# Joining the two runs of small matmuls of each head in a hybrid decoder step

## The chip, the cores and the metric

One core of one Trainium2 chip. The metric is the device time of one execution in microseconds (us), on the slowest core used, here the only one.

## The reference

One inference step of one decoder layer over 512 prompt tokens and 8 sample tokens (one new token for each of 8 sequences), model width 1024, all in float32. The layer has an HGRN2 branch (8 heads, keys and values of 128), an RG-LRU branch, a gated merge, and a feed-forward part of width 4096. What the change touches is HGRN2 alone:

```python
S_t = diag(f_t) S_{t-1} + k_t outer v_t,   o_t = S_t^T q_t          # per head, S is 128 x 128
# chunkwise, per chunk of the prompt:
A = einsum('bhtk,bhsk,bhtsk->bhts', qc, kc, decay)     # s <= t, decay = product of f between s and t
o = o_inter + einsum('bhts,bhsv->bhtv', A, vc)
```

For the prompt, the masked matrix A of each chunk of 128 tokens is wanted. For the 8 sample tokens, one step: the stored state is scaled by f, k outer v is added, and q is applied.

## The kernel before

Big products are float32 done as three rounded products (`products`, L112, instruction at L118): a weight tile of 128 columns is split by ScalarE (L84, the high part) and VectorE (L87, the low part), and one product of 128 output columns takes 48 matmuls of 260 columns into a PSUM tile of the pool pmm, of which there are two. Splits are made two weights ahead. `gemm` also emits the gates of RG-LRU that are pending (`blockdiag`, L779, which reads xcs, the split of xc, which the conv chain L793 to L797 makes), and whatever parts have been put off with `later(n, part)`: they are emitted after the n-th next product.

Heads come one after another, each with six big products: f, q, output gate and v of the head (`head`, L530), and two for RG-LRU. After the v product, `head_sample_v` (L557) transposes the sample part of v, stores it to DRAM (vd, L564) and loads it back broadcast over all partitions (vb, L566), both on the DMA queue of SyncE.

`head_prompt` (L586) builds A by levels. `level(b)` (L609) for b = 1, 2, 4 up to 64 makes from the level before it two rows of factors, q-like and k-like, multiplied by decay factors, by one VectorE multiply (L614) and one copy (L618; for b = 1 the copy is ScalarE's, L616). Levels 1 to 32 go to tiles named Y, of which RING = 4 are alive; level 64 overwrites X, the head's own q, k and q times f. Blocks of A with distance between b and 2b are products of a level's two rows. For small b they are 32 x 32 blocks on the diagonal, computed whole by `blocks` (L633) and selected by masks. `small` (L626) issues one such matmul of 32 output columns, with high priority (`SESSION`), ordered behind the one before it, so that the small ones of one run stand together on TensorE. A small matmul is two MATMUL entries in the trace.

There are two runs in each head:

- Run 1, 48 matmuls behind level 2: the diagonal and level 1 from X (L647, 64 columns each), and the blocks for 2 and 4. VectorE then multiplies by the diagonal's mask (L650) and selects levels 1, 2 and 4 (copy_predicated, L652) into a32.
- Levels 4 to 32 follow, then `head_sample` (L570): ScalarE scales the eight stored states (L573) and VectorE adds k outer v from vb (L574), in eight updates ordered behind level 32. Level 64 is ordered behind the last.
- Run 2, 56 matmuls, ordered behind level 64's copy (order alone): level 64's block from the level 32 tile (L665), the sample outputs from the states st (L669), the blocks for 8 and 16, and the block for 32 (L674). VectorE then selects levels 8 and 16 (L676), and ScalarE copies the other blocks into `at` (L678, L681) and the sample outputs out (L682).

The keys' transposes (L694) come three products later, the states' products (L704) and outputs (L717, L719) one product later each.

The order of each engine's instructions is fixed when the program is built: a planner takes estimated durations, and gives each engine the ready instruction of the highest priority next. An order dependency made with `behind` only fixes this order; data dependencies become semaphore waits on the chip. GpSimd's own DMA queue keeps its descriptors in a scratch area of each SBUF partition.

Of the kernel before, what the change touches and what calls it, by code (L numbers as in the profile page):

```python
# [6 lines left out]
F32 = mybir.dt.float32  # L7
# [4 lines left out]
OP = mybir.AluOpType  # L12
# [10 lines left out]
C = 128  # L23
NC = L // C
# [16 lines left out]
PAIR = "pair"  # L41
EARLY = 8
EARLY_PLACE = 4
RING = 4
FIRST = 3
BUFS = {"e": 6, "g": 6, "xb": 1, "xc": 2, "xcs": 2, "gate": 4, "ag": 2, "hs": 3, "y": 3, "ma": 8, "rs": 1, "sq": 1, "t": 6, "sqs": 2,
        "a": 16, "b": 16}
# [4 lines left out]
class Kernel:  # L52
# [533 lines left out]
    def head_prompt(self, h, f, X, q, v, og, st, vb, fkq):  # L586
        nc = self.nc
# [11 lines left out]
        a32 = self.hg.tile([128, NC, 32], F32, name="a32")  # L599
        at = self.at  # L600

        def view(t, first_q, first_k, step, n, b):

            return bass.AP(tensor=t.tensor, offset=t.offset + first_q,
                           ap=[t.ap[0], [T + first_k - first_q, 2], [step, n], [1, b]])

        levels, decay = [X], [f[:, :L], 0]

        def level(b):  # L609

            X, (tb, to), n = levels[-1], decay, L // (2 * b)
            Y = levels[0] if b == C // 2 else self.hg.tile([128, 2, T], F32, name="Y", bufs=RING)
            fac = bass.AP(tensor=tb.tensor, offset=tb.offset, ap=[tb.ap[0], [1, 2], [2, n], [0, b]])
            made = nc.vector.tensor_tensor(view(Y, b, 0, 2 * b, n, b), view(X, b, 0, 2 * b, n, b), fac, OP.mult)  # L614
            if b == 1:
                nc.scalar.copy(view(Y, 0, 1, 2, n, 1), view(X, 0, 1, 2, n, 1))  # L616
            else:
                made = nc.vector.tensor_copy(view(Y, 0, b, 2 * b, n, b), view(X, 0, b, 2 * b, n, b))  # L618
            t2 = tb.rearrange("p (n two) -> p n two", two=2)
            tn = T_[:, to:to + n]  # L620
            nc.vector.tensor_tensor(tn, t2[:, :, 0], t2[:, :, 1], OP.mult)
            levels.append(Y)
            decay[:] = tn, to + n
            return made

        def small(after, *args):  # L626
            with self.tc.high_priority(offset=SESSION):
                ins = nc.tensor.matmul(*args, start=True, stop=True)  # L628
            for x in after:
                self.behind(ins, x)  # L630
            after[:] = [ins]

        def blocks(after, p, c0, x):  # L633
            for c in range(NC):
                for j in range(4):
                    s = slice(c * C + 32 * j, c * C + 32 * j + 32)
                    small(after, p[32 * j:32 * j + 32, c0 + c * 32:c0 + c * 32 + 32], x[:, 1, s], x[:, 0, s])
            return p[:, c0:c0 + 128].rearrange("p (c t) -> p c t", c=NC)

        level(1)  # L640
        made = [level(2)]
        p = self.pps.tile([128, 512], F32, name="ps")
        for c in range(NC):
            for j in range(4):
                s = c * C + 32 * j
                o = p[32 * j:32 * j + 32, c * 64:c * 64 + 64].rearrange("p (x t) -> p x t", x=2)
                small(made, o, X[:, 1, s:s + 32], X[:, 0::2, s:s + 32])  # L647
        first = p[:, :256].rearrange("p (c x t) -> p c x t", c=NC, x=2)
        found = {1: first[:, :, 0], 2: blocks(made, p, 256, levels[1]), 4: blocks(made, p, 384, levels[2])}
        nc.vector.tensor_tensor(a32, first[:, :, 1], self.mdiag, OP.mult)  # L650
        for b in (1, 2, 4):
            nc.vector.copy_predicated(a32, self.masks[b], found[b])  # L652

        level(4)
        level(8)
        level(16)
        state = self.head_sample(h, st, vb, fkq, level(32))
        with self.urgent():
            made = [self.behind(level(64), state)]
        p = self.pps.tile([128, 512], F32, name="ps")  # L660
        p2 = self.ppt.tile([128, 512], F32, name="pt")
        for c in range(NC):
            for j in (0, 32):
                s = c * C
                small(made, p2[j:j + 32, c * 64:c * 64 + 64], levels[6][:, 1, s + j:s + j + 32],  # L665
                      levels[6][:, 0, s + 64:s + 128])
        for b in range(NB):
            j, c = 32 * (b % 4), 256 + 128 * (b // 4)
            small(made, p2[j:j + 32, c:c + 128], fkq[:, 2], st[:, b])  # L669
        found = {b: blocks(made, p, c0, levels[n]) for b, c0, n in ((8, 0, 3), (16, 128, 4))}  # L670
        for c in range(NC):
            for j in (0, 64):
                s = c * C + j
                small(made, p[j:j + 32, 256 + c * 32:288 + c * 32], levels[5][:, 1, s:s + 32], levels[5][:, 0, s + 32:s + 64])  # L674
        for b in (8, 16):
            nc.vector.copy_predicated(a32, self.masks[b], found[b])  # L676
        for j in (0, 64):
            nc.scalar.copy(at[j:j + 32, :, j + 32:j + 64], p[j:j + 32, 256:384].rearrange("p (c t) -> p c t", c=NC))  # L678
# [4 lines left out]
        X, tb = levels[-1], decay[0]  # L683
# [1010 lines left out]
def build(inputs):  # L1694
    import numpy as np
    import concourse.bacc as bacc

    nc = bacc.Bacc("TRN2", target_bir_lowering=False, num_devices=1)
    arrays, ins, outs = {}, {}, {}
    for name in _INS:  # L1700
        a = np.ascontiguousarray(inputs[name])
        arrays[f"in_{name}_dram"] = a
        ins[name] = nc.dram_tensor(f"in_{name}_dram", a.shape, mybir.dt.from_np(a.dtype), kind="ExternalInput").ap()
    for n, (name, shape) in enumerate(_OUTS):
        outs[name] = nc.dram_tensor(f"out_{n}_dram", shape, F32, kind="ExternalOutput").ap()
    with tile.TileContext(nc, schedule_with_timeline_sim=True) as tc, ExitStack() as ctx:
        Kernel(ctx, tc, ins, outs).run()
    return nc, arrays
# [8 lines left out]
```

## Time and profile before

| | |
|---|---|
| median of 3 runs | 1008.83 us (1008.13 to 1009.62) |
| the profiled execution, its own time | 1009.9 us |
| its span, first to last instruction | 1008.1 us |
| TensorE busy | 983.1 us, 98% |
| VectorE busy | 695.9 us, 69% |
| ScalarE busy | 515.6 us, 51% |
| small matmuls (L628) on the chain that ended last | 1% on ps tiles, 1% on pt tiles |

In the profile PE is TensorE's matmul, PEld its weight load, DVE VectorE, ACT ScalarE, POOL GpSimd, SP SyncE. A q behind an engine's name means its sequencer or its DMA issue. A row of the timeline gives start, length, engine, line, operation, output and inputs, shape and count, and in brackets the idle time of the engine before it with what ended it. Matmuls are pipelined, so the lengths of neighbours overlap, and starts tell more than lengths.

### The profile page before, as it was taken

The page shows a single profiled execution, that of the slowest core. Times are in us where ns is not written, and L with a number is a line of the kernel's source. Part 1 is how long each engine was busy: PE and PEld are TensorE (multiplying, and loading weights), DVE is VectorE, ACT ScalarE, POOL GpSimd, SP SyncE. Part 2 cuts the span into 40 slices and gives each one's busy share as a digit, 9 for nine tenths or more (in the row PEclk, how much of TensorE's full clock was granted, in tenths as well). Part 3 has the DMA queues.
Part 4 walks back from the last instruction along what each step waited for, and adds up shares of the span by engine and source line. Part 5 has one row for each costly group of instructions (what it writes and reads, how often), then busy time and mean ns, then how long its engine had stood idle before and what let it go on. Part 6 is the DMA issues. An engine that isn't in the chain of part 4 may idle for free.

```text
span 1008.1 us, 23268 instructions
## 1 busy us (share of the span) xinstructions
PE 983.1 (98%) x9585; PEld 956.5 (95%) x9585; DVE 695.9 (69%) x1548; ACT 515.6 (51%) x986; POOL 112.6 (11%) x194
## 2 busy tenths in 40 slices
PE   5999999999999999999999999999999999999996
PEld 3799999999999999999998999999999999999996
DVE  6768888698878868463233338667767776777686
ACT  5444764574565456351122224466555645656664
POOL 3000000000000000120000000022321331232151
PEclk9899999999999999999999999999999999999998
DMA  9794444354444434586666756322762483274242
GB/s 301 214 259 135 121 129 149 94 147 131 113 126 122 119 94 131 186 267 210 190 189 195 241 165 181 99 85 53 155 170 64 98 197 104 54 170 93 63 85 85
DMA packets 212572, 145.78 MB, mean 145 GB/s; under 512 B 6262, under 2 KB 196878, under 8 KB 212458
## 3 DMA queue, kind: packets, MB, share of 16 engines
q1 hardware_dynamic: 202562, 132.37, 44.5%
q0 software_dynamic: 9904, 11.92, 6.3%
q8 instruction: 75, 1.23, 0.5%
q14 instruction: 31, 0.25, 0.1%
HBM read 123.61 MB, written 13.39 MB: 136 GB/s over the span
## 4 chain that ended last, share of the span: by engine, by line
PE 90%; DVE 3%; DMA 3%; SPq 2%; ACT 1%; issue 1%; DVEq 0%; ACTq 0%
PE mm L118 65%; PE ps L1151 8%; PE pt L1151 4%; PE ps L382 2%; PE pb L1151 2%; PE pb L779 1%; PE ps L628 1%; DMA wm<-in_w_mod_dram 1%; PE pt L704 1%; DMA xT_d<-ma 1%; SPq L75 1%; PE pt L717 1%; DMA wst<-in_w_in_dram 1%; DMA vb<-vd 1%; PE pt L628 1%
## 5 line engine op out<-in xcount | busy, mean ns | idle before, releaser
L118 PE MATMUL mm<-h,whi 128*128 128x260 f32 (+1 forms) x3072 | 508.3, 285 | 1.9 <-ACT X L157 1.2
L118 PEld LDWEIGHTS mm<-h,whi 128*128 128x128 f32 x3072 | 426.2, 189 | 6.7 <-ACT whi L84 1.7
L118 PE MATMUL mm<-h,wlo 128*128 128x260 f32 (+1 forms) x1536 | 314.6, 284 | 0.0
L84 ACT CAST whi<-wst 128x1024 fp32r<-128x1024 f32 x166 | 173.6, 1048 | 208.1 <-PE mm L118 171.2
L87 DVE TENSOR_TENSOR wlo<-wst,whi 128x1024 fp32r<-128x1024 f32 x166 | 202.6, 1221 | 90.4 <-ACT whi L84 89.3
L118 PEld LDWEIGHTS mm<-h,wlo 128*128 128x128 f32 x1536 | 239.8, 189 | 0.1
L118 PE MATMUL mm<-a,whi 128*128 128x260 f32 x512 | 82.8, 283 | 0.0
L118 PEld LDWEIGHTS mm<-a,whi 128*128 128x128 f32 x512 | 70.3, 188 | 0.9 <-issue 0.8
L118 PE MATMUL mm<-a,wlo 128*128 128x260 f32 x256 | 51.7, 284 | 0.0
L1247 DVE TENSOR_TENSOR f<-f 128x260 f32<-128x260 f32 x64 | 27.3, 427 | 28.9 <-ACT f L1242 28.2
L880 POOL DMA_DIRECT2D t<-oaT_d x8 | 4.3, 551 | 375.8 <-PE mm L118 368.8
L1239 POOL TENSOR_TENSOR ft<-ft,fsh 128x8 f32<-128x8 f32 x28 | 18.5, 660 | 215.5 <-DVE ft L1233 215.5
L1236 ACT ACTIVATE ft<-ft,fsh 128x512 f32<-128x512 f32 (+2 forms) x36 | 24.0, 676 | 35.9 <-DVE ft L1233 35.9
L118 PE MATMUL mm<-b,whi 128*128 128x260 f32 x256 | 41.6, 284 | 0.0
L118 PEld LDWEIGHTS mm<-a,wlo 128*128 128x128 f32 x256 | 39.4, 188 | 0.0
L118 PEld LDWEIGHTS mm<-b,whi 128*128 128x128 f32 x256 | 35.0, 188 | 2.5 <-issue 2.5
L614 DVE TENSOR_TENSOR Y<-Y,tb 128x512 f32<-128x512 f32 x40 | 27.5, 688 | 11.0 <-ACT Y L616 5.5
L896 DVE TENSOR_TENSOR t<-mm,t 128x520 f32<-128x520 f32 x8 | 5.6, 700 | 37.0 <-PE mm L118 37.0
L1284 POOL DMA_DIRECT2D ma<-snap x28 | 26.5, 948 | 40.1 <-issue 22.3
L1263 POOL DMA_DIRECT2D ma<-snap x28 | 26.6, 950 | 38.6 <-DMA ma<-snap 22.8
L1242 ACT ACTIVATE f<-ft 128x520 f32<-128x520 f32 (+1 forms) x36 | 20.8, 587 | 15.0 <-POOL ft L1240 13.0
L573 ACT ACTIVATE st<-st,fkq 128x128 f32<-128x128 f32 x64 | 19.6, 389 | 13.9 <-DVE fkq L553 12.8
(477 smaller groups left out, 1824.0 us busy)
## 6 DMA issues: line engine op xcount, KB each, us to landing
wst<-in_w_in_dram SPq DMA_DIRECT2D x64, 512.0 KB
wm<-in_w_mod_dram SPq DMA_DIRECT2D x8, 2048.0 KB
wst<-in_w_ff_dram SPq DMA_DIRECT2D x64, 256.0 KB
wst<-in_w_ff_dram SPq DMA_DIRECT2D x32, 512.0 KB
wm<-in_w_mod_dram SPq DMA_DIRECT2D x8, 1024.0 KB
st<-in_state_hgrn_dram SPq DMA_DIRECT2D x8, 512.0 KB
vb<-vd SPq DMA_DIRECT2D x8, 512.0 KB
out_dram<-st SPq DMA_DIRECT2D x8, 512.0 KB
```

The lines of the kernel that those rows point to most:

```text
L84: ins = self.nc.scalar.copy(hi, st)
L87: ins = self.nc.vector.tensor_tensor(lo, st, hi.bitcast(F32), OP.subtract)
L118: self.last_product = self.nc.tensor.matmul(ps[:, s, :c.stop - c.start], x, y[:, c], start=first and n == 0, stop=last and n == 2)
L382: ins = nc.tensor.matmul(ps[r:r + 32, j * n:j * n + n], self.cT[:, k, :], w[:, k, :], start=k < 4, stop=k >= KO - 4)
L614: made = nc.vector.tensor_tensor(view(Y, b, 0, 2 * b, n, b), view(X, b, 0, 2 * b, n, b), fac, OP.mult)
L628: ins = nc.tensor.matmul(*args, start=True, stop=True)
L1151: ins = self.nc.tensor.matmul(ps, x[:, w], y[:, f], start=j in (1, 7, 2) and k == 0 and n == 0, stop=k == 3 and n == 2, skip_group_check=True)
L1236: nc.scalar.activation(t[:, :p], t[:, :p], AF.Relu, bias=sh[:, 0:1])
L1242: nc.scalar.activation(f, self.two(self.ft)[:, a:a + n], AF.Square)
L1247: self.nc.vector.tensor_tensor(f[:, n], f[:, a], f[:, b], op)
L1263: nc.gpsimd.dma_start(x[1][:, b], v[:, :n], accum_op=OP.add)
L1284: nc.gpsimd.dma_start(x[t][:, a], s[p], accum_op=OP.add)
```

## The change

Run 1's matmuls move behind the state update and become one run with run 2's: first level 64's block, then the sample outputs, then the diagonal and level 1, the blocks for 2, 4, 8 and 16, and the block for 32. The run is ordered behind the last state update only, no longer behind level 64; level 64 is emitted behind the run (it overwrites X, which the run reads). The multiply by the diagonal's mask and all five selections come behind it. So six level tiles must be alive at once: RING goes from 4 to 6, and the scratch area of GpSimd's DMA queue is set to 8192 bytes a partition to make room.

```diff
-RING = 4
+RING = 6
+SCRATCH = 8192
...
-        level(1)
-        made = [level(2)]
-        p = self.pps.tile([128, 512], F32, name="ps")
-        for c in range(NC):
-            for j in range(4):
-                s = c * C + 32 * j
-                o = p[32 * j:32 * j + 32, c * 64:c * 64 + 64].rearrange("p (x t) -> p x t", x=2)
-                small(made, o, X[:, 1, s:s + 32], X[:, 0::2, s:s + 32])
-        first = p[:, :256].rearrange("p (c x t) -> p c x t", c=NC, x=2)
-        found = {1: first[:, :, 0], 2: blocks(made, p, 256, levels[1]), 4: blocks(made, p, 384, levels[2])}
-        nc.vector.tensor_tensor(a32, first[:, :, 1], self.mdiag, OP.mult)
-        for b in (1, 2, 4):
-            nc.vector.copy_predicated(a32, self.masks[b], found[b])
-
-        level(4)
-        level(8)
-        level(16)
+        for b in (1, 2, 4, 8, 16):
+            level(b)
         state = self.head_sample(h, st, vb, fkq, level(32))
-        with self.urgent():
-            made = [self.behind(level(64), state)]
-        p = self.pps.tile([128, 512], F32, name="ps")
+        made = [state]
         p2 = self.ppt.tile([128, 512], F32, name="pt")
...
-        found = {b: blocks(made, p, c0, levels[n]) for b, c0, n in ((8, 0, 3), (16, 128, 4))}
+        p = self.pps.tile([128, 512], F32, name="ps")
+        for c in range(NC):
+            for j in range(4):
+                s = c * C + 32 * j
+                o = p[32 * j:32 * j + 32, c * 64:c * 64 + 64].rearrange("p (x t) -> p x t", x=2)
+                small(made, o, X[:, 1, s:s + 32], X[:, 0::2, s:s + 32])
+        first = p[:, :256].rearrange("p (c x t) -> p c x t", c=NC, x=2)
+        found = {1: first[:, :, 0], 2: blocks(made, p, 256, levels[1]), 4: blocks(made, p, 384, levels[2])}
+        p = self.pps.tile([128, 512], F32, name="ps")
+        found |= {b: blocks(made, p, c0, levels[n]) for b, c0, n in ((8, 0, 3), (16, 128, 4))}
...
-        for b in (8, 16):
+        with self.urgent():
+            self.behind(level(64), state)
+        nc.vector.tensor_tensor(a32, first[:, :, 1], self.mdiag, OP.mult)
+        for b in (1, 2, 4, 8, 16):
             nc.vector.copy_predicated(a32, self.masks[b], found[b])
...
-    nc = bacc.Bacc("TRN2", target_bir_lowering=False, num_devices=1)
+    nc = bacc.Bacc("TRN2", target_bir_lowering=False, num_devices=1, dynamic_dma_scratch_size=SCRATCH)
```

## The prediction

> **What bounds the kernel now.** I read the page first (share of each engine, the chain that ended last), then busy time by stretch, then the waits of TensorE, and then the timeline around the two runs of small matmuls.
>
> ```profile
> PE 983.1 (98%) x9585; PEld 956.5 (95%) x9585; DVE 695.9 (69%) x1548; ACT 515.6 (51%) x986; POOL 112.6 (11%) x194
> ```
> ```profile
> PE 90%; DVE 3%; DMA 3%; SPq 2%; ACT 1%; issue 1%; DVEq 0%; ACTq 0%
> ```
>
> TensorE is the bound: 98% of the span, 90% of the chain. The stage of the change is the eight heads, from about 43 to 400 us. Columns below: stretch, length, then each engine's busy time.
>
> ```profile
> 66.00:86.00 20.00, 19.22 (x341) 18.60 (x339) 13.62 (x37) 6.42 (x12) 0.00 (x0) 1.00 0.62 173
> 86.00:110.00 24.00, 24.00 (x202) 24.00 (x203) 21.52 (x61) 15.02 (x39) 0.00 (x0) 1.00 0.36 101
> ...
> 130.00:400.00 270.00, 269.63 (x3338) 267.08 (x3338) 221.10 (x593) 155.25 (x332) 0.00 (x0) 1.00 0.42 122
> ```
>
> From 86 us on TensorE has no gap worth the name (269.63 of 270), so a microsecond taken off it there is a microsecond of the result, and so is one in which it waits. The one gap between 66 and 86 us (0.78) is this wait, whose matmul starts at 85.90:
>
> ```profile
> 85.90 0.39 PE L779 MATMUL pb<-xcs,bdhlru_wa 128*128 128x260 f32 x1 [0.78 <-ACT xcs L183]
> ```
>
> VectorE is at 82% in 130 to 400 us (221.10 of 270): busy, not the bound.
>
> **The change, part by part. The edges of a run.** Head 0's two runs on TensorE (start, length, line, count; one small matmul is two entries):
>
> ```profile
> 68.93 0.52 PE L118 MATMUL mm<-h,whi 128*128 128x260 f32 x3
> 69.38 0.65 PE L628 MATMUL ps<-X 128*32 128x64 f32 x32
> 69.85 0.74 PE L628 MATMUL ps<-Y 128*32 128x32 f32 x64
> 70.53 0.39 PE L118 MATMUL mm<-h,whi 128*128 128x260 f32 x1
> 70.75 0.40 PE L118 MATMUL mm<-h,wlo 128*128 128x260 f32 x2
> ...
> 80.11 0.28 PE L118 MATMUL mm<-h,wlo 128*128 128x260 f32 x1
> 80.31 0.58 PE L628 MATMUL pt<-Y 128*32 128x64 f32 x14
> ...
> 80.79 0.61 PE L628 MATMUL pt<-st,fkq 128*32 128x128 f32 x14
> 81.15 1.16 PE L628 MATMUL ps<-Y 128*32 128x32 f32 x80
> 82.24 0.39 PE L118 MATMUL mm<-h,wlo 128*128 128x260 f32 x1
> 82.46 0.64 PE L118 MATMUL mm<-h,whi 128*128 128x260 f32 x4
> ```
>
> In the big products one matmul follows another every 0.12 us (202 in 24.00 us from 86 to 110 us). Three of these at 68.93 put the last at 69.17, and the run starts 0.21 later. Within it the small ones start every 0.011 us (96 from 69.38 to 70.39, the last being 0.20 long). From the last small one to the next big one passes 0.14, and from that to the one after it 0.22 (70.53 to 70.75). The edges so take 0.21 + 0.14 + 0.22 = 0.57 us. Without the run two ordinary steps of 0.12 and, in the joined run, one small step of 0.01 stand there: 0.25. Run 2's edges are alike (0.20, 0.13, 0.22). **Joining saves 0.32 us a head, 2.5 us over eight.** The 104 small matmuls themselves stay as they are, in another order. I see no reason for another price: from both sides 0.25 to 0.40 a head (2.0 to 3.2).
>
> **Where the joined run lands.** Today run 2 is ordered behind level 64's copy; the new one only behind the last state update, and it takes the first run's work with it. So the state update now decides when 104 matmuls go, and TensorE stops there if the state is late. VectorE in head 0:
>
> ```profile
> 66.77 0.28 DVE L562 COPY vs<-ps 8x128 f32<-8x128 f32 x1 [2.22 <-PE ps L560]
> ```
> ```profile
> 74.37 0.42 DVE L618 COPY Y<-Y 128x512 f32<-128x512 f32 x1
> 77.32 0.62 DVE L574 SCALAR_TENSOR_TENSOR st<-vb,fkq,st 128x128 f32<-128x128 f32 x2 [2.53 <-DMA vb<-vd]
> 77.85 0.30 DVE L652 COPY_PREDICATED a<-mask,ps 128x128 f32<-128x128 uint8 x1
> 78.05 1.66 DVE L574 SCALAR_TENSOR_TENSOR st<-vb,fkq,st 128x128 f32<-128x128 f32 x6
> ```
> ```profile
> 82.77 0.41 DVE L618 COPY X<-Y 128x512 f32<-128x512 f32 x1
> ```
>
> The order was planned with vb there when level 32 was done (74.79, end of the first L618 row); on the chip it came 2.53 us later, and all VectorE work behind it slid. Run 2, planned behind level 64's copy, started at 80.31, while that copy ended at 83.18; less the 2.53 it would have ended at 80.65. So plan and chip agree within 0.34 us but for that DMA. Today it costs no wait at run 2, because the run does not really need the copy, and its place was late enough for the state (79.71).
>
> In the joined kernel the state can be planned sooner: level 16 no longer waits for run 1 to free its buffer (six buffers), the mask selections are gone from between the updates, so vb alone sets it. Planned end of the state: vb at 74.8 or before, plus eight updates. They take 2.2 us here (77.32 to 79.71 less a 0.2 mask selection), so 77.0 or before. On the chip vb stays at 77.3 (its issue, below, hangs on weight loads and not on the run), so the state ends at 79.5. The last small matmul that reads it stands 0.8 us into the run (80.31 to 81.15), so the stall is 79.5 - (77.0 + 0.8) = 1.7 us at least. At most: vb planned as soon as the later heads have it, which is 6.8 us after the issue of vd:
>
> ```profile
> 67.08 0.29 SPq L564 DMA_DIRECT2D vd<-vs  x1
> 71.28 0.53 SPq L566 DMA_DIRECT2D vb<-vd  x1
> ```
> ```profile
> 112.41 0.33 SPq L564 DMA_DIRECT2D vd<-vs  x1
> 114.80 0.34 SPq L566 DMA_DIRECT2D vb<-vd  x1
> ```
> ```profile
> 119.21 0.61 DVE L574 SCALAR_TENSOR_TENSOR st<-vb,fkq,st 128x128 f32<-128x128 f32 x2
> ```
>
> 67.08 + 6.8 = 73.9, so 0.9 sooner, and up to 0.9 more if the plan is more hopeful than any head: a stall of 3.5. From the other side, nothing if other VectorE work is put ahead of the updates. I take 2.3, near the end that rows give. Of it 0.8 comes back: the matmul at 85.90 today waits 0.78 for the slid chain, and a TensorE 2.3 us later no longer does. **Head 0 pays 2.3 - 0.8 = 1.5 us.**
>
> **Heads 1 to 7.** In head 1 vb landed by 119.21, at most 6.8 us after vd was issued, against 10.2 in head 0 (later issue, slower transfer) and against the at most 7.7 that the plan trusted there. VectorE waited for vb once only (row below). So I take nothing here. From the other side: if the plan trusts vb as much too early as in head 0, each pays 2.5 - 0.8 = 1.7 us, 12 us in all.
>
> ```profile
> DVE st L574 <- DMA vb<-vd: 2.5, 1, 2.5
> ```
> ```profile
> DVE Y L614 <- PE ps L628: 5.5, 6, 1.5
> ```
>
> **The rest, beside TensorE.** The last row is the wait of level 16 for run 1; it goes. In its place level 64, which overwrites X, waits for the joined run's 32 entries that read X: they end some 1.3 us into the run (0.84 for the first two groups, 0.47 for these), so about 1.3 us a head instead of 0.9. Behind it on VectorE stand weight splits and the conv chain; the splits run two weights ahead (two big products, 11.6 us), so nothing. K, level 64's product, is transposed not before the third big product after the head's last; today its copy ends at 83.18, 2.9 us after run 2 begins, and only the last head waits for it:
>
> ```profile
> PE pt L694 <- DVE X L618: 0.4, 1, 0.4
> ```
>
> The new copy comes some 3 us after the start of an earlier run (an estimate: 1.3, then a multiply and a copy), so nothing, or that 0.4 again. The mask selections (five of 0.30, and one multiply) move behind the run; their reader, the output product, stands five big products behind the head. ScalarE's copy of p behind them waits today already; its cover is the second accumulator, one big product of 48 matmuls, 5.8 us. The two ps banks are held together; their next user is the next head. The smaller DMA scratch touches GpSimd's queue only: it is idle in this stage, and in the feed-forward part TensorE does not wait for it, so nothing.
>
> **Sum.** -2.5 + 1.5 = -1.0 us. Against the profiled execution's 1009.9 (span 1008.1) that is 1008.9; that execution is 1.1 above the median 1008.83, so I predict 1007.8. 0.2% (2 us) is about what this measurement tells from no change.
>
> **Rivals.** *Full gain:* the update is planned late enough, because VectorE is at 82% and its other work goes first; head 0 does not wait and the 0.8 at 85.90 partly goes: -2.5 to -3.2, 1006.0. For it: in head 0 today's state ends 0.6 us before run 2 (79.71, 80.31) in spite of its late vb. Against it: the high priority with which these matmuls are placed.
>
> *Slower, the state is late in the later heads:* place, the first matmul on st; price 1.7 us each as above; it decides from 0.15 us a head to undo the forecast, from 0.45 to make the kernel slower by 2 us; 1010.9 to 1020. For it: freed of the buffer wait, every head's update now hangs on vb alone, as head 0's does today. Against: vb is quicker there than in head 0 by 3.4 us.
>
> *Slower, the clock.* TensorE's granted clock fell after its pause at the start (the column behind the brackets):
>
> ```profile
> 20.00:24.00 4.00, 1.42 (x28) 0.59 (x20) 4.00 (x9) 2.96 (x6) 0.00 (x0) 1.00 1.14 321
> 24.00:28.00 4.00, 1.97 (x13) 1.20 (x17) 4.00 (x12) 1.10 (x2) 0.00 (x0) 0.62 1.09 349
> 28.00:31.00 3.00, 3.00 (x29) 1.41 (x22) 2.68 (x9) 1.83 (x4) 0.00 (x0) 0.50 1.09 348
> 31.00:35.00 4.00, 4.00 (x36) 3.78 (x40) 2.01 (x10) 1.59 (x4) 0.00 (x0) 0.90 1.09 347
> ```
>
> Some 4.6 us idle in eight (2.58 and 2.03) were followed, and overlapped, by half clock for 3.0 + 3.0 + 0.8 = 6.8 us, 3.4 us of work lost. If head 0's stall comes near 3.5 and sets that off: -2.5 + 3.5 - 0.8 + 3.4 = +3.6, 1012.4. The Trainium skill ("TensorE: Matmul & The Clock Gate", Part 1: The HAM clock gate) has the rate halved after one idle window of about 3.4 us; by that rule my 2.3 us sets off nothing and only the longest stall would. The trace agrees in kind, with its idle time broken up.
>
> *No gain at the edges:* the joined run is broken up by big matmuls while single updates are awaited; each break costs the 0.32 again: 1008.8 or a little over. Today's run 2 is whole in spite of the same eight updates.
>
> **How the numbers follow.** Forecast (head 0 takes back over half; edges broken up in part belongs here): 0.43, 1006.8 to 1009.5. Full gain: 0.32, 1005.6 to 1006.8. Late states: 0.17. Clock: 0.08. So faster 0.32, same 0.43, slower 0.25. Range 1005.6 to 1012.4: it leaves out the greater part of the late states and little else. The forecast's own range is 1006.8 to 1009.5.
>
> **What would show it.** One run of 208 entries a head instead of 96 and 112; TensorE's busy time less by some 2.5 us; a new TensorE wait at a matmul on st in head 0 of 1.7 to 3.5 us, with an idle VectorE ahead of it waiting for vb; none at 85.90. VectorE's wait for run 1 gone, one at level 64 instead. It is wrong if waits on st show up in several heads, or none in head 0, or if the edges of the joined run cost more than 0.57.

## The result and the profile after

| | before | changed |
|---|---|---|
| median | 1008.83 us (1008.13 to 1009.62) | 1025.74 us (1023.47 to 1029.83) |
| span of the profiled execution | 1008.1 us | 1025.9 us |

The changed kernel is slower: the ratio is 1.0171 (95% interval 1.0156 to 1.0186), 17 us. The forecast was 1007.8 with a range to 1012.4. It was wrong, and by a mechanism that none of its rivals named.

The page of the changed kernel: busy time, TensorE's granted clock in 40 slices, and the queue that brings instructions (packets, MB, share).

```profile
PE 986.0 (96%) x9585; PEld 959.2 (94%) x9585; DVE 694.0 (68%) x1548; ACT 515.6 (50%) x986; POOL 112.0 (11%) x194
PEclk9999999999899998999999999999999999999998
q8 instruction: 75, 1.23, 0.5%
```

TensorE executes the same number of instructions as before and is busy about as long (983.1 before), so the 17.8 us of span are time in which it stood still or ran on a lower clock. The stage says where. Columns as in the prediction:

```profile
66.00:86.00 20.00, 17.75 (x316) 16.31 (x314) 14.10 (x37) 6.27 (x11) 0.00 (x0) 1.00 0.68 185
...
130.00:400.00 270.00, 262.00 (x3286) 259.71 (x3289) 211.93 (x577) 150.61 (x323) 0.00 (x0) 0.99 0.42 121
```

From 130 to 400 us TensorE had 0.4 us idle before and has 8.0 now. Its waits (what was waited for, total, times, longest):

```profile
PE ps L629 <- issue: 10.2, 4, 4.2
...
PE pt L690 <- DVE tb L622: 1.3, 2, 1.0
PE pt L629 <- issue: 1.3, 1, 1.3
...
PE pb L775 <- ACT xcs L184: 1.0, 1, 1.0
```

The first row is new and the largest part of the matter. L629 is the small matmul, and "issue" says that TensorE waited for nothing that the profile shows: no semaphore, no operand. The four places on the timeline, in heads 2, 3, 4 and 7, with the rows ahead of two of them:

```profile
171.38 0.93 PE L629 MATMUL ps<-Y 128*32 128x32 f32 x76
173.06 0.88 PE L629 MATMUL ps<-Y 128*32 128x32 f32 x66 [0.75 <-issue]
...
224.99 0.57 PE L629 MATMUL ps<-Y 128*32 128x32 f32 x30 [1.27 <-issue]
...
260.18 1.49 PE L629 MATMUL ps<-Y 128*32 128x32 f32 x135
265.62 0.42 PE L629 MATMUL ps<-Y 128*32 128x32 f32 x7 [3.95 <-issue]
...
406.26 0.42 PE L629 MATMUL ps<-Y 128*32 128x32 f32 x6 [4.23 <-issue]
```

Each lies in the middle of matmuls on tiles of the same names; by the run's order in the program the matmul just before the stop was reading the same level (the blocks for 8, 16, 32 and 32). In head 4 only 7 of the run's 208 MATMUL rows are left when it comes. Heads 1, 5 and 6 run through without a stop. The two long stops are followed by a lower clock (the column behind the brackets; each row begins where a stop ends):

```profile
265.60:272.50 6.90, 6.88 (x40) 6.82 (x40) 1.48 (x6) 1.26 (x4) 0.00 (x0) 0.57 0.02 4
...
406.20:413.10 6.90, 6.84 (x42) 6.78 (x43) 2.70 (x7) 2.53 (x5) 0.00 (x0) 0.62 0.12 42
```

That costs 6.9 x 0.43 + 6.9 x 0.38 = 5.6 us of work. The account: stops 10.2, clock 5.6, the late state in head 0 1.3 + 1.3 (below), the waits at L690 0.9 more than at the same transposes before (1.3, 0.4), less the 2.5 forecast for the edges: +16.8 of the 17.8. The rest was not followed up.

**Two theories.** Instructions reach TensorE by the queue q8: 75 packets of 1.23 MB in all, so 16.4 KB each. TensorE's 9585 + 9585 entries in 75 packets are 256 to a block, 64 bytes each. A small matmul in float32 is two matmul and two weight-load entries: a run of 104 is 416 entries of this stream (entries count both from here on). The big products use 2 x 202 entries in 24 us (17 per us, a block in 15 us), a run that is not stopped 416 in 2.85 us (146 per us).

- *F (feeding):* the run outpaces the blocks. Counted in the trace's records (with TensorE's 82 semaphore and drain instructions), all four stops fall at the same place modulo 256, at 192 to within one entry. Each ends 1.3 to 1.5 us after a block of q8 has landed, by the queue's packet times: in head 2 the block landed 0.5 us before the stop began, in head 3 as it began; in head 4 it starts 1.4 us into the stop, at 263.02, lands at 264.14, and TensorE resumes at 265.62; in head 7 the three times are 403.73, 404.79 and 406.26. A run of 192 or 224, as before, never used up what had landed. By the counts, with k blocks landed, TensorE gets to entry 256k + 448 and no further, so whether a run of 416 passes depends on where in a block it starts: it should pass from about 185 to 255 and from 0 to 32 (modulo 256), and stop elsewhere unless the block comes early.
- *S (the run itself):* the joined run, its six level tensors or an operand or transfer in just these heads stops TensorE; the number of entries and their place in the blocks do not matter.

The Trainium skill ("Runtime: NRT & Kernel Launch", Instruction fetch mechanics) describes refills in blocks of 16 KiB, 256 instructions, and the trace agrees (16.4 KB, 256). It also holds that fetching is hidden because dispatch is slower than the refill; at some 150 entries per us the trace disagrees, by 10.2 us.

### The profile page after: what moved, and what is told of

Same layout as the page of the kernel before. It is cut to its first block, busy times and chain, and to the rows that moved or that the text cites. A ratio compares the mean times of both kernels' runs of the same rounds, so it can differ in the third digit from the quotient of the medians.

```text
span 1025.9 us, 23249 instructions
## 1 busy us (share of the span) xinstructions
PE 986.0 (96%) x9585; PEld 959.2 (94%) x9585; DVE 694.0 (68%) x1548; ACT 515.6 (50%) x986; POOL 112.0 (11%) x194
## 3 DMA queue, kind: packets, MB, share of 16 engines
q8 instruction: 75, 1.23, 0.5%
## 4 chain that ended last, share of the span: by engine, by line
PE 85%; DVE 5%; DMA 4%; SPq 3%; issue 2%; ACT 0%; DVEq 0%; ACTq 0%
PE mm L119 62%; PE ps L1147 8%; PE pt L1147 4%; PE pb L1147 2%; PE ps L383 2%; SPq L372 2%; DMA wm<-in_w_mod_dram 1%; DMA vb<-vd 1%; PE pb L775 1%; PE ps L629 1%; DVE wlo L88 1%; SPq L76 1%; PE pt L713 1%; PE pt L700 1%; DMA xT_d<-ma 1%
## 5 line engine op out<-in xcount | busy, mean ns | idle before, releaser
L158 ACT ACTIVATE gate<-pb,pa 128x260 f32<-128x260 f32 x32 | 15.3, 477 | 25.9 <-PE pb L775 25.7
```

## The experiments

Each is compared with runs of the kernel before on the same chip (medians 1009.3, 1010.0 and 1009.4 us in the three groups).

### A shorter joined run

The changed kernel without the blocks for 2 and 4, so 288 entries in a run; their part of A is left out.

```diff
-        found = {1: first[:, :, 0], 2: blocks(made, p, 256, levels[1]), 4: blocks(made, p, 384, levels[2])}
+        found = {1: first[:, :, 0]}
...
-        for b in (1, 2, 4, 8, 16):
+        for b in (1, 8, 16):
             nc.vector.copy_predicated(a32, self.masks[b], found[b])
```

> The joined run without the blocks for 2 and 4 (that part of A is left out): 72 matmuls a head, 288 entries of TensorE's stream instead of 416. Theory F (instruction blocks): TensorE's instructions come in 16 KB blocks of 256 entries on DMA queue q8, and in the changed kernel it stopped each time 64 entries short of a block's end, when the next block was late; a run of 288 is hardly longer than the 284 to 404 that it did without a stop. So the four waits inside the run (10.2 us) and the two stretches at half clock behind the long ones (6.8 us) go, and the work left out is 8 x 64 x 0.011 = 5.6: 1025.7 - 22.6 = 1003 us, between 1001.5 and 1006. Theory S (the run waits for data: a level's tile, a PSUM bank, the late states): the blocks for 8, 16 and 32, in which it stopped, are all still there with what they read, so the waits stay and only the work goes: 1020 us.

Measured: 1008.28 us (1007.27 to 1010.27), ratio 0.9989 (0.9979 to 0.9999). The four stops are gone; of what is left of TensorE's waits at the heads' work in this kernel, the two longest and one inside a run:

```profile
PE pt L629 <- issue: 1.5, 1, 1.5
PE pb L775 <- ACT xcs L184: 1.5, 1, 1.5
...
PE ps L629 <- issue: 0.5, 1, 0.5
```
```profile
342.00:349.00 7.00, 5.54 (x31) 5.34 (x32) 6.40 (x20) 2.35 (x6) 0.00 (x0) 0.76 0.28 77
```

The first is head 0's late state (on pt, at the state's products). The last is a short stop inside a run, in head 7, again at 192 modulo 256: the run starts at 173, and by F's count 275 of its 288 entries were at hand until the block that landed at 389.73. S fails: the blocks for 8, 16 and 32, where the stops were, are all there, and so are the six tensors. F is right on the four stops and some 5 us too low on the total, outside its range (to 1006). Part of that is in these rows: TensorE now waits 1.5 us for ScalarE's xcs in head 6, and behind that wait the clock fell (7.0 x 0.24 = 1.7 us).

### A longer second run in the kernel before

The two runs and the four level tensors of before, and 48 repeated matmuls at the end of run 2, into columns that nothing reads; run 2 so has 416 entries.

```diff
             for j in (0, 64):
                 s = c * C + j
                 small(made, p[j:j + 32, 256 + c * 32:288 + c * 32], levels[5][:, 1, s:s + 32], levels[5][:, 0, s + 32:s + 64])
+        for _ in range(3):
+            blocks(made, p, 384, levels[4])
```

> The kernel before with its two runs, and behind run 2 of each head 48 repeated matmuls (the blocks for 16, three times, to spare columns of PSUM), so that run 2 has 416 entries of the stream, as the joined run has; no order around it is changed. Work added: 8 x 96 x 0.011 = 8.4 us. Theory F: run 2 now starts, counted modulo 256 in TensorE's stream, at 236, 61, 8, 71, 20, 83, 32, 91 for heads 0 to 7; a run of 416 that starts between about 33 and 185 must stop for a block. So heads 1, 3, 5 and 7 stop at 192 (modulo 256), 1.5 to 4 us each, heads 0, 2, 4 do not, head 6 is on the edge; with one to four stretches at half clock (3.4 each): 1017 + 6 to 16 + 0 to 14, 1023 to 1040, most likely 1030. Theory S: these matmuls read tiles that are done and wait for nothing: 1017.2 us, no wait inside the runs.

Measured: 1039.19 us (1036.96 to 1042.27), ratio 1.0300 (1.0279 to 1.0320). The instruction queue, the waits put down to issue, and the stops of this kernel:

```profile
q8 instruction: 81, 1.33, 0.5%
```
```profile
PE ps L628 <- issue: 10.0, 4, 3.1
...
PE mm L118 <- issue: 3.0, 2, 2.0
PE pb L781 <- issue: 2.0, 1, 2.0
```
```profile
138.37 0.44 PE L628 MATMUL ps<-Y 128*32 128x32 f32 x14 [2.28 <-issue]
...
178.94 1.97 PE L628 MATMUL ps<-Y 128*32 128x32 f32 x176
...
184.54 0.40 PE L118 MATMUL mm<-h,wlo 128*128 128x260 f32 x2 [1.99 <-issue]
...
233.88 0.51 PE L628 MATMUL ps<-Y 128*32 128x32 f32 x19 [3.08 <-issue]
...
328.30 0.41 PE L628 MATMUL ps<-Y 128*32 128x32 f32 x25 [2.89 <-issue]
...
423.75 0.45 PE L628 MATMUL ps<-Y 128*32 128x32 f32 x29 [1.79 <-issue]
```

Heads 1, 3, 5 and 7 stop inside the run; their long runs start at 60, 70, 82 and 90. Heads 0, 2, 4 and 6 (235, 7, 19, 31) get through it, as 178.94 shows for head 2. But heads 2, 4 and 6 stop right behind the run, for 2.0, 1.0 and 2.0 us, at the same 192 modulo 256 (the two lower waits, and the row of 184.54). The expectation did not have these stops; the count 256k + 448 does. The queue confirms the unit too: 8 x 48 x 4 = 1536 more entries are six blocks of 256, 81 against 75. So the length alone does it, without the join. F's range was 1023 to 1040, S's time 1017.2.

### The joined run placed, and misplaced

The join as in the change, with each head's run, and where needed its keys, pinned between chosen big products. In the kernel *placed* all eight start inside F's window (189, 195, 223, 188, 208, 212, 240, 192); in *misplaced* all stand at the one place (2, 5) and start at 57, 221, 223, 109, 103, 245, 239, 91.

```diff
+PLACE = ((3, 7, 1, 1), (2, 5), (2, 5), (4, 2, 0, 6), (3, 7, 1, 1), (2, 5), (2, 5), (4, 1, 0, 6))   # placed
+PLACE = ((2, 5),) * 8                                                                              # misplaced
...
+                if self.mid and self.mid[0][0] == (self.ngemm, k):
+                    self.mid.pop(0)[1]()
...
+        self.mid.append(((self.ngemm + PLACE[h][0], PLACE[h][1]), run))
```

> The joined run with all its 416 entries, but its place is chosen: it is emitted in the middle of the third, fourth or fifth big product after the head, so that it starts at 190, 196, 224, 189, 209, 213, 241, 193 modulo 256 in TensorE's stream, just behind the landing of a block. Theory F: no stop inside any run, no state late (the places are later than in the changed kernel), the joining saves 0.32 a head: 1008.8 - 2.5 = 1006.3 us, between 1005 and 1008.5. Theory S: the tiles and banks that the run shares are as in the changed kernel, so at least the waits inside it stay: 1015 us or more. If the edges were worth nothing: 1008.8.

> The same as the placed kernel, but every run in the middle of the third product after its head: starts at 58, 222, 224, 110, 104, 246, 240, 92 modulo 256. Theory F: heads 0, 3, 4 and 7 stop at 192 (modulo 256), 1.5 to 4.3 us each, heads 1, 2, 5 and 6 do not: the placed kernel's time plus 6 to 16, plus 3.4 for each stop near 4 us: 1013 to 1032, most likely 1020. Theory S: within 2 us of the placed kernel.

Measured: *placed* 1010.40 us (1009.73 to 1012.47), ratio 1.0014 (1.0005 to 1.0023); *misplaced* 1026.15 us (1023.83 to 1028.32), ratio 1.0163 (1.0142 to 1.0183). Stops of *misplaced*, heads 0, 1, 3, 4, 5 and 7:

```profile
84.42 0.54 PE L632 MATMUL ps<-Y 128*32 128x32 f32 x13 [2.58 <-issue]
...
135.59 1.14 PE L632 MATMUL ps<-Y 128*32 128x32 f32 x94 [1.15 <-issue]
...
226.79 0.64 PE L632 MATMUL ps<-Y 128*32 128x32 f32 x38 [1.61 <-issue]
...
267.33 0.60 PE L632 MATMUL ps<-Y 128*32 128x32 f32 x35 [1.54 <-issue]
...
321.89 0.60 PE L699 MATMUL pt<-ident,X 128*128 128x128 f32 x4 [3.07 <-ACT whi L86]
...
408.04 0.57 PE L632 MATMUL ps<-Y 128*32 128x32 f32 x29 [3.04 <-issue]
```

Heads 0, 3, 4 and 7 are the four outside the window. Head 1's start (221) is inside, and it stopped all the same: the block due before the run landed only at 134.19, 1.8 us into it. So the window holds only where the block is in time. The row of 321.89 is not in a run: it is the keys' transpose 6 us behind head 5's. The view names a split of ScalarE's, but the transpose does not read it; the stop is at 192 modulo 256 and ends 1.5 us after a block's landing, so it is put here with F's. One more of 1.1 us stands behind head 1's run. *Placed* has no stop in any run; its stretch 130 to 400 us holds 269.46 us of TensorE's work in 270. One of its runs in whole, in head 2:

```profile
171.07 0.58 PE L632 MATMUL pt<-Y 128*32 128x64 f32 x14
...
172.38 1.61 PE L632 MATMUL ps<-Y 128*32 128x32 f32 x142
173.93 0.39 PE L784 MATMUL pb<-xcs,bdhlru_wa 128*128 128x260 f32 x1
```

From its first matmul to the next big one it takes 2.86 us; the two runs of before take 1.15 + 1.93 = 3.08 (head 0: 69.38 to 70.53 and 80.31 to 82.24, rows in the prediction). That is 0.22 saved, with one edge into a run (0.21 less 0.12) 0.31, and with the slow step behind the first big matmul (0.22 less 0.12) 0.41, against the forecast's 0.32. Over whole heads less is left: from head 1's run to head 5's *placed* takes 173.78 us (130.32 to 304.10), the kernel before from run 2 to run 2 174.49 (124.44 to 298.93), 0.18 a head; TensorE is idle for 0.46 us of it in *placed*, and not at all before. *Placed* is still not faster than before, and misses both forecasts: F's range ended at 1008.5, S's began at 1015. Its loss stands in head 0:

```profile
PE mm L120 <- ACT xb L795: 1.8, 1, 1.8
```
```profile
84.00:88.00 4.00, 4.00 (x23) 4.00 (x22) 4.00 (x9) 1.55 (x4) 0.00 (x0) 0.57 0.19 56
```

VectorE waits for vb, the conv chain stands behind the state update, ScalarE's copy xb behind that, and TensorE behind the copy; then the clock is lower for 4 us (1.7 us). 1.8 + 1.7 - 2.5 = +1.0 with the forecast's edges, and +2.1 with 0.18 a head; measured are 1.1 between the medians. The link from wait to clock is read from the trace's order, not tested.

### Head 0 left as it was, and the ring alone

*head0_apart* keeps two runs in head 0, run 2 pinned behind the second big product, and joins the others in F's window. *ring_alone* is the kernel before with RING = 6 and the smaller scratch, and nothing else.

```diff
+        if h:
+            self.mid.append(((self.ngemm + PLACE[h][0], PLACE[h][1]), run))
+        else:
+            apart()      # the two runs of before
```
```diff
-RING = 4
+RING = 6
+SCRATCH = 8192
```

> Head 0 keeps two runs, as in the kernel before; the joined runs of heads 1 to 7 start where the blocks of instructions are due to suffice (entry counts of 187 to 239, modulo 256). In the kernel named placed a joined run took 2.85 us where the two of before took 1.15 + 1.92, that is 0.22 us less for a head, and head 0's late state alone cost it 1.8 us at a copy of ScalarE's and 1.7 us of lower clock behind that. Theory F (instruction supply alone made the joined runs dear): no stop inside a run, no wait of 1 us or more on the copy, no half clock before 110 us, and 7 x 0.22 = 1.5 us off the time of the kernel before, about 1007.7 us, ratio 0.9985 (0.997 to 1.0). Rival S (a joined run, or six level tensors, is dear in itself): 1010 us or more, ratio above 1.001, with the loss spread over the heads' stage.

> The kernel before with its two runs for each head, and only the sixth level tensor and the smaller descriptor scratch that makes room for it. The larger ring lets the order begin head 0's second run 5 us sooner, in five pieces, behind the state tensor's products, so each piece adds an edge of 0.57 us at most and head 0 may wait some 1 to 2 us for the state. Theory F: no stop inside a run in heads 1 to 7, 1008 to 1012 us, ratio 0.999 to 1.003. Rival S (the six tensors or the scratch cost the 17 us): above 1020 us.

Measured: *head0_apart* 1018.17 us (1016.75 to 1019.83), ratio 1.0080 (1.0065 to 1.0095); *ring_alone* 1020.31 us (1018.86 to 1021.01), ratio 1.0099 (1.0082 to 1.0116). Both miss my numbers, and by its numbers S had both right: 1010 us or more for *head0_apart*, above 1020 us for the ring. But S had the loss spread over the heads, or all 17 us of it, and the rows below show most of it in one or two places. No run of the two kernels has a stop inside it, except head 0's wait for the state in *ring_alone*. Of *head0_apart*, the two waits, and the clock around and behind each:

```profile
PE mm L120 <- ACT xb L851: 2.8, 1, 2.8
...
PE mm L120 <- issue: 2.0, 2, 1.8
```
```profile
84.00:92.00 8.00, 7.37 (x135) 7.02 (x136) 7.36 (x24) 5.27 (x13) 0.00 (x0) 0.59 0.52 144
141.00:150.00 9.00, 7.17 (x47) 6.96 (x46) 6.93 (x16) 3.31 (x6) 0.00 (x0) 0.81 0.36 106
```

The xb wait was moved, not removed, and the clock behind it cost 8.0 x 0.41 = 3.3 us. The 1.8 us stop is F's, at 192 modulo 256, but it ends 5.6 us behind the run and lies in big products: head 1's run had used up the lead, and the next block landed at 142.49, TensorE going on at 143.98. So a run that passes can still stop what follows it. Of *ring_alone*:

```profile
74.00:80.00 6.00, 3.00 (x30) 1.75 (x29) 3.27 (x10) 0.00 (x0) 0.00 (x0) 0.87 0.26 91
80.00:88.00 8.00, 8.00 (x112) 5.60 (x113) 4.46 (x14) 1.84 (x4) 0.00 (x0) 0.67 0.46 131
```

With six tensors the order starts head 0's run 2 at 74.54, before the state (80.31 in the kernel before), broken up by big matmuls: TensorE idle for 3.0 us of 6, then on two thirds of its clock. Counted by the n-th big product, it is 7.7 us behind the kernel before at 88 us, and 10.4 at 420 us. So the tensors cost by the order they allow, mostly in head 0; *placed* has them too, at +1.1 us. Ring and scratch were not run apart.

### The same program, shifted by 152 entries

The changed kernel with 38 matmuls at the start, in TensorE's wait for c; nothing else. This is the sharpest test: order, operands and run length are untouched, and only the place of each run in the blocks moves.

```diff
         ps = self.ppt.tile([128, 512], F32, name="pt")
+        for _ in range(38):
+            nc.tensor.matmul(ps[:32, 256:288], self.ident[:, :32], self.ident[:, :32], start=True, stop=True)
```

> The changed kernel, with 38 matmuls of 32 columns added (their results are not used) at the very start, where TensorE waits 3.1 us for the tile c; nothing else. By theory F they are 152 entries of TensorE's instruction stream, so every later run starts 152 entries later in its block: heads 1 to 7 at 108, 61, 245, 198, 126, 79, 197 (modulo 256) in place of 213, 166, 94, 47, 231, 184, 46. A run of 416 stops where its start lies outside 185 to 255 and 0 to 32. Theory F: the stops of heads 3, 4 and 7 vanish, head 1, 2, 5 and 6 have one each, 64 entries short of a block's end (192 modulo 256), of 0.7 to 4.2 us; the total depends on these lengths and on the clock behind them, 1017 to 1035 us. Rival S (something in heads 2, 3, 4 and 7 themselves stops them: a late operand, a transfer, the length of the run): the same four heads stop, for the same times, and 1024 to 1028 us.

Measured: 1024.56 us (1023.28 to 1026.93), ratio 1.0153 (1.0136 to 1.0169). The instruction queue, and the four stops, heads 1, 2, 5, 6; between them head 4's last row, where the changed kernel stood for 3.95 us:

```profile
q8 instruction: 76, 1.25, 0.5%
```
```profile
135.95 0.64 PE L631 MATMUL ps<-Y 128*32 128x32 f32 x38 [1.19 <-issue]
...
174.86 0.44 PE L631 MATMUL ps<-Y 128*32 128x32 f32 x14 [2.27 <-issue]
...
262.84 1.61 PE L631 MATMUL ps<-Y 128*32 128x32 f32 x142
...
315.23 0.70 PE L631 MATMUL ps<-Y 128*32 128x32 f32 x47 [1.13 <-issue]
...
354.70 0.75 PE L631 MATMUL ps<-Y 128*32 128x32 f32 x23 [2.80 <-issue]
```

The clock behind the stop of 2.80 us:

```profile
354.70:358.70 4.00, 4.00 (x38) 3.94 (x39) 2.20 (x9) 0.87 (x3) 0.00 (x0) 0.50 0.01 4
358.70:363.00 4.30, 4.30 (x30) 4.30 (x29) 0.47 (x1) 1.53 (x3) 0.00 (x0) 0.76 0.00 0
```

The stops are in exactly the four heads that F names, all at 192 modulo 256; heads 3, 4 and 7 pass, head 7's run 0.3 us longer than the others. S said the same heads as in the changed kernel. The time alone would not tell, as it lies in both ranges; the heads settle it for F.

### Placed once more

The joined runs again in the window (with 27 matmuls at the start), head 0's just ahead of the product that had waited for xb.

```diff
+PLACE = ((2, 7), (4, 5, 0, 6), (4, 2, 0, 6), (2, 5), (2, 5), (4, 4, 0, 6), (4, 2, 0, 6), (2, 5))
```

> The joined runs again placed where theory F lets them pass (starts at 189, 196, 217, 241, 215, 202, 235, 215, by 27 unused matmuls at the start and by the position between the big products), with head 0's run put just ahead of the product that in the kernel named placed waited 1.8 us for ScalarE's copy, so that the run fills that wait. Theory F: no stop inside a run; if head 0's state (ready at about 79.2 us) is in time, no wait over 1 us at head 0, no half clock there, and 8 x 0.22 = 1.8 us less than before: 1007.5 us, ratio 0.998 (0.997 to 1.0015, the upper end if head 0 still waits). Rival S (a joined run is dear in itself, or in most heads): 1015 us or more.

Measured: 1014.48 us (1013.78 to 1015.46), ratio 1.0049 (1.0036 to 1.0063). No stop inside a run, and none of 1 us on xb; the wait went elsewhere, and work in 130 to 400 us is at 266.72 of 270:

```profile
PE pb L786 <- ACT gate L161: 2.2, 2, 1.8
```

So the forecast for this placement failed, though not on the stops inside the runs. Two shorter stops stand behind the runs of heads 5 and 6 (0.6 and 0.7 us, ending 1.4 and 1.5 us after a block's landing, at 193 and 194 modulo 256). What the rest is was not followed up. No complete version of the join that was run beats the kernel before; the 2.5 us forecast for the edges is less than what each tried order loses elsewhere.

## Why the prediction was wrong

- **The edges: about right in size, wrong as the whole price.** 0.41 us a head by the rows of one run where nothing stops, 0.18 over whole heads (forecast 0.32, range 0.25 to 0.40). The step that failed is the sentence behind it, "The 104 small matmuls themselves stay as they are, in another order. I see no reason for another price". The price came from runs of 192 and 224 entries, and I carried it over to 416 without asking whether the instructions arrive at that rate. The missing term is 10.2 us of stops and 5.6 us of clock.
- **Half of it was there to be read before:** the page's q8 row, 75 blocks for 2 x 9585 entries, and run 1's own rows, 96 matmuls and as many weight loads in 1.15 us, where a block lasts 15 us in big products. How far ahead the blocks land the page does not give; by the packet times and the count above, 207 to 529 more entries were at hand when a run began, in all these traces. A rival could have been made of it, with a bound from both sides: nothing where a run of 416 finds enough, a stop for a late block where it does not.
- **Head 0's late state: right.** Two rows of the changed kernel, of VectorE and TensorE:

```profile
76.63 2.19 DVE L575 SCALAR_TENSOR_TENSOR st<-vb,fkq,st 128x128 f32<-128x128 f32 x8 [3.13 <-DMA vb<-vd]
```
```profile
77.08 1.93 PE L629 MATMUL pt<-st,fkq 128*32 128x128 f32 x14 [1.27 <-issue]
```

  TensorE stood 1.27 us, and then took 1.93 us for 14 MATMUL rows that took 0.61 in the kernel before (row of 80.79 in the prediction), since it went from update to update: 1.3 more, 2.6 us in all (forecast 2.3, range 1.7 to 3.5). Big matmuls stand within the run, as in the rival *no gain at the edges*, in this head alone. The 0.8 us at pb did not come back: it is 1.0 now.
- **Heads 1 to 7, "nothing" for a late state: right.** VectorE does wait for vb now in seven heads, as that rival had it:

```profile
DVE st L575 <- DMA vb<-vd: 12.9, 7, 3.2
```

  but TensorE waits for st in none of heads 1 to 7, because the run comes later than the state there. What these heads lose are the stops, which the term did not mean.
- **The clock rival:** the fall came, but behind the stops of heads 4 and 7, not of head 0, and at its size: 6.9 us at about half, twice (forecast 6.8 us at half). Across the kernels the fall follows the length of a stop only roughly. Single stops and waits up to 1.6 us were followed by none, but in *less_blocks* waits of 1.5 and 0.4 us close together were. Most of 1.8 to 3.2 us were followed by half clock for some 3.4 us, two by none (1.8 us in *placed_again*, 2.0 in *padded*), two by about 6.8 us (2.8 us in *head0_apart*, and in *shifted*, rows of 354.70 and 358.70), as were the two near 4 us and, in *ring_alone*, waits of 2.0 and 1.0 us close together. The Trainium skill ("TensorE: Matmul & The Clock Gate", Part 1) has one idle window of about 3.4 us halve the rate; here stops shorter than that (1.8 to 3.2 us) did it too, so it was no safe ground for "my 2.3 us sets off nothing".
- **Ring and scratch, "nothing":** wrong by itself (+10 us in *ring_alone*), mostly by the order that the ring allows in head 0.

## What to carry to other kernels

Before making a dense run of small instructions longer, count its entries (four for a small float32 matmul here) and set them against the instruction queue: blocks, their size, and how far ahead they land. Here runs of 192 and 224 entries never stopped, one of eight runs of 288 stopped for 0.5 us, 416 stopped in half the heads of the changed kernel, and 152 entries added at the start changed which heads. A wait put down to "issue" within matmuls on one tile is the sign to look for; a stop of some 2 us or more mostly costs again by the clock behind it. And a run that passes can leave the stop to the big products behind it.

## What was not expected of the hardware

- TensorE stopped at 192 modulo 256 (to within one entry) in every such stop in a run, 64 entries short of a block's end, and resumed 1.2 to 1.6 us after the next block had landed. Why 64 short is open.
- A block's transfer takes about 1.1 us, but began up to 4.5 us after the run's first matmul (399.20, 403.73 in head 7): the stops of the changed kernel last 0.75 to 4.23 us. What delays the block is open.
- 38 unused matmuls at the start move stops of up to 4 us from some heads to others 130 to 400 us later.
